# Cumulative sums stored by chunks, larger transfers, and merge loads begun by GpSimd, in a hybrid SSD and attention layer

## The chip, the cores and the metric

The kernel runs on one core of one Trainium2 chip. A core has a matrix engine (TensorE, PE, whose weight loads the profile lists as PEld), three engines that work elementwise (VectorE, DVE; ScalarE, ACT; GpSimd, POOL), and SyncE (SP), which here only begins transfers. Transfers between the chip's memory (DRAM) and the core's (SBUF) run on 16 DMA engines; any of SP, ACT and POOL can begin them, each through a queue of its own, in the order of its program. The metric is the device time of one execution in microseconds, as a median over runs.

## What is computed

One decoder layer on x of 1024 tokens by 1024 channels, in float32: a Mamba-2 branch (SSD) and a latent attention branch (MLA) side by side, merged by sigmoid gates, then a gated MLP with a short convolution.

```python
h = rms_norm(x, norm_mix_g)
z, xbc, dt_raw, q_a, kv_a, k_rope_raw, gates = split(h @ w_in)
y_ssd = ssd_mixer(z, xbc, dt_raw, ...) @ w_ssd_proj      # 32 heads in 4 groups, 8 chunks of 128 tokens
y_mla = mla_mixer(q_a, kv_a, k_rope_raw, ...) @ w_mla_proj  # 16 heads, causal
g_ssd, g_mla = split(sigmoid(gates + gate_b))
x = x + (g_ssd * y_ssd + g_mla * y_mla) @ w_o
u_gate, u_val = split(causal_conv(rms_norm(x, norm_ffn_g) @ w_up))
x = x + (silu(u_gate) * u_val) @ w_down

# in ssd_mixer, per chunk and head
a_cum = cumsum(dt * a)                                   # along the 128 tokens of a chunk
decay_in = exp(where(causal, a_cum[l] - a_cum[s], -inf))
y_diag = einsum(scores, decay_in, x * dt)
y_off = einsum(C, state before the chunk, exp(a_cum))
```

## The kernel before, in words

Matrix products are made exact enough by splitting each float32 operand into a high part (rounded to float32r) and a remainder: three matmuls (high x high, high x low, low x high; lines 174 to 176) stand for one. For weights, `load_w` brings a matrix in two halves: SP loads a half into `wraw` (two buffers, line 159), ACT casts it to `whi` (line 152), and POOL or DVE subtracts to get `wlo` (line 153). `whi` and `wlo` have two buffers too, so the loads run only a little ahead of PE. Activations (`h`) are split in the same way (lines 145 to 153).

The stages, by time in the profile:

- 0 to 100 us: norm, the small projections, and the cumulative sums of dt times a. These stand in SBUF as `acum` (tokens on partitions); a transposed copy (32 heads by 1024 tokens) goes to DRAM as `ac_d` (line 521).
- to 700 us: attention, eight pairs of heads in two halves of 512 queries. Gate and z projections are fitted in between from the table `PACE`, and stored in DRAM as `g_d` and `z_d` (line 306, out of `lt`, lines 328 and 329). The unnormalised attention output goes to `at_d`, the inverse row sums to `l_d` (line 685 ff.).
- to about 1285 us: SSD, four groups of eight chunks. For each chunk ACT begins `abc_load` (line 788), which broadcasts the chunk's cumulative sums of the group's eight heads to all 128 partitions (`abc`, 128 x 1024), and `z_load` (line 796). ACT makes the decays `seg` from `abc` (lines 850 and 852), DVE multiplies them (lines 863 to 867), PE makes the state `sn` (line 874) and the output `yp` (line 891). Besides, the convolutions (lines 808 to 816), the normalising of `at_d` by `l_d` (lines 977 to 988), and from about 1150 us on the attention projection (`mla_tiles`) run in the background: 16 tiles, each with a gate load (line 1028, into buffers `rb` or `chan`, five in turn) and a store to `m_d` (line 1035).
- to about 1570 us: the merge, in two halves of 512 tokens. For each of eight tiles `ct`, ACT begins the loads of `gt` from `g_d` and `mt` from `m_d`; PE multiplies by `w_ssd` (48 matmuls of 512 columns), DVE gates and adds (lines 1223, 1224, 1228). Then `w_o`, the residual x, and the store of `x2_d`. `w_raw` begins the loads of the first MLP weights, `ur` (512 KB each, lines 1126 and 1127), whose sums POOL makes (lines 1147 to 1150).
- to the end: the MLP.

The code is recorded first; a scheduler then sets each engine's order, and `behind(name)` adds a constraint that the last recorded instruction comes after another one of its engine. Each engine then runs its instructions in order, DMA issues included.

Of the kernel before, what the change touches and what calls it, by code (L numbers as in the profile page):

```python
# [9 lines left out]
F32 = mybir.dt.float32  # L10
# [7 lines left out]
P = 128  # L18
T = 1024
NT = T // P  # L20
# [4 lines left out]
HEADS = 32  # L25
GROUPS = 4
MH = 16
FFT = 22
# [44 lines left out]
def tile_hybrid_layer(ctx: ExitStack, tc: tile.TileContext, x, cols, cons, w_main, w_small, w_uq, w_ukv,  # L73
                      w_ssd, w_mla, w_o, w_up, w_down, out, pace=PACE):
    nc = tc.nc
# [6 lines left out]
    hp = ctx.enter_context(tc.tile_pool(name="hp", bufs=16))  # L82
    pl = ctx.enter_context(tc.tile_pool(name="pl", bufs=2, space=PSUM))

    ac_d = dram.tile([HEADS, T], F32, name="ac_d")
    at_d = dram.tile([D, T], F32, name="at_d")
    l_d = dram.tile([MH, T], F32, name="l_d")
    y_d = dram.tile([2 * D, T], F32, name="y_d")
    z_d = dram.tile([2 * D, T], F32, name="z_d")
    g_d = dram.tile([2 * D, T], F32, name="g_d")  # L90
# [35 lines left out]
    def behind(name):  # L126

        ins = nc.cur_bb.bb.instructions[-1]
        if name:
            tc.add_manual_dep(ins, name, mybir.DependencyInfo(  # L130
                mybir.DependencyClass.NoSync, mybir.DependencyReason.DATA), reason="order")
        return ins.name

    def last(engine):
        return [ins for ins in nc.cur_bb.bb.instructions if ins.engine == engine][-1].name
# [379 lines left out]
    for half in range(2):  # L515
# [2 lines left out]
        for i in range(4):  # L518
            PE.transpose(ps[0:32, i * P:(i + 1) * P], acum[:, half * 4 + i, :], ident)
        S.copy(act_[:, hs_(half)], ps[0:32, :])  # L520
    nc.sync.dma_start(out=ac_d, in_=act_)
    bctx.close()


    with tc.tile_pool(name="cp", bufs=2) as cp, tc.tile_pool(name="pss", bufs=4, space=PSUM) as pss, \
# [146 lines left out]
        def output(pr, half, accs, pv):  # L672

            ps = bank()
            for c in range(4):
                PE.matmul(ps[32 * c:32 * c + 32, 0:256], lhsT=ones[:, 0:32],
                          rhs=accs[c // 2][:, (c % 2) * 256:(c % 2) * 256 + 256], start=True, stop=True)
            ao = cp.tile([P, 512], F32, name="ao", bufs=1)
            S.copy(ao, pv)
            nc.sync.dma_start(out=at_d[pr * P:(pr + 1) * P, hs_(half)], in_=ao)  # L680
            lr = cp.tile([P, 512], F32, name="e", bufs=6)
            S.copy(lr[0:97, 0:256], ps[0:97, 0:256])
            for c in range(4):
                a = half * 512 + (c % 2) * 256
                nc.sync.dma_start(out=l_d[2 * pr + c // 2, a:a + 256], in_=lr[32 * c:32 * c + 1, 0:256])

        def chain(*gens):
            for g in gens:
# [83 lines left out]
    with tc.tile_pool(name="dp", bufs=2) as dp, tc.tile_pool(name="psx", bufs=1, space=PSUM) as psx, \  # L772
# [10 lines left out]
        def abc_load(n):  # L783

            if n < GROUPS * NT:
                g, c = divmod(n, NT)
                t = dp.tile([P, 8, P], F32, name="abc", bufs=3)
                nc.scalar.dma_start(out=t, in_=ac_d[8 * g:8 * g + 8, c * P:(c + 1) * P].partition_broadcast(P))
                abcs.append(t)

        def z_load(n):
# [181 lines left out]
        def normalize(n):  # L973


            if stores:
                nc.sync.dma_start(out=stores[0][0], in_=stores[0][1])
                stores.pop()
            if loaded:
                raw, rb, dst = loaded.pop()  # L980
                G.tensor_tensor(raw, raw, rb, op=ALU.mult)
                behind(squared[0])
                stores.append((dst, raw))
            if n < 16:
                k, s = n // 2, hs_(n % 2)
                raw = dp.tile([P, 512], F32, name="rb", bufs=3)
                rb = dp.tile([P, 512], F32, name="nb")
                nc.sync.dma_start(out=raw, in_=at_d[k * P:(k + 1) * P, s])
                for hd in range(2):
                    nc.sync.dma_start(out=rb[64 * hd:64 * hd + 64, :], in_=l_d[2 * k + hd, s].partition_broadcast(64))  # L990
                loaded.append((raw, rb, at_d[k * P:(k + 1) * P, s]))

        def mla_tiles():

            at1 = []
            count = [0]

            def at1_step(j):

                if j % 4 == 2 and 6 <= j < 38:  # L1000
                    at1.append(ordered_split(staged.pop(0)))
                if j % 4 == 0 and j < 32:
                    staged.append(raw_load(at_d, j // 4, hs_(1), lt.tile([P, 512], F32, name="lt")))

            def y_step(j):

                if 8 <= j < 16 and j % 2 == 0:
                    ya0[j // 2 - 4] = ordered_split(staged.pop(0))
                if 25 <= j:
                    ya0[j - 21] = ordered_split(staged.pop(0))  # L1010
                if j < 24 and j % 2 == 0:
                    k = j // 2
                    raw = dp.tile([P, 512], F32, name="nb") if 4 <= k < 6 else \
                        dp.tile([P, 8, P], F32, name="abc", bufs=3).rearrange("p a b -> p (a b)")[:, 0:512] if k > 8 else \
                        lt.tile([P, 512], F32, name="lt")
                    staged.append(raw_load(y_d, k, hs_(0), raw))

            def one(w, ct, half, side=None):
                s = hs_(half)

                n = turn[0] = turn[0] + 1
                gt = dp.tile([P, 512], F32, name="rb", bufs=3) if n % 5 < 3 else \
                    dp.tile([P, T], F32, name="chan", bufs=4)[:, 0:512]
                ps = lin_tile()
                for k, _ in enumerate(steps([w], (at, at1)[half], ps, range(KD), KD)):
                    if k == 2:
                        name = last(mybir.EngineType.SP)
                        nc.sync.dma_start(out=gt, in_=g_d[(8 + ct) * P:(9 + ct) * P, s])
                        behind(name)
                    if side:  # L1030
                        side(count[0])
                    count[0] += 1
                    yield True
                V.scalar_tensor_tensor(gt, gt, 1.0, ps, op0=ALU.add, op1=ALU.mult)
                nc.sync.dma_start(out=m_d[ct * P:(ct + 1) * P, s], in_=gt)

            for ct in range(4):
                w = load_w(w_mla[ct], [P, KD, P])
                if held:
                    name = last(mybir.EngineType.SP)  # L1040
                    release()
                    behind(name)
                yield from one(w, ct, 0, at1_step)
            for ct in range(4, 8):
                w = load_w(w_mla[ct], [P, KD, P])
                for half in range(2):
                    yield from one(w, ct, half, at1_step)
            count[0] = 0
            for ct in range(4):
                yield from one(load_w(w_mla[ct], [P, KD, P]), ct, 1, y_step)  # L1050
            ya0[11] = ordered_split(staged.pop(0))
# [11 lines left out]

        abc_load(0)
        ls = dp.tile([P, P], F32, name="bt")
        lv = l_d.rearrange("h (c t) -> (h c) t", t=P)
        for n, _ in enumerate(conv_group(0)):

            if n == 17:
# [50 lines left out]
    class Pair:  # L1120
        e = None

    def w_raw(q):
        q.r1 = up.tile([P, KD, P], F32, name="ur1", bufs=2)
        q.r2 = up.tile([P, KD, P], F32, name="ur2", bufs=2)
        nc.sync.dma_start(out=q.r1, in_=w_up[q.j])
        nc.sync.dma_start(out=q.r2, in_=w_up[FFT + q.j])

    def w_tiles(n, wide=True):
        if n < 2:  # L1130
# [37 lines left out]
    with tc.tile_pool(name="ep", bufs=2) as ep:  # L1168
        x2b = []
        with tc.tile_pool(name="em", bufs=2) as em:  # L1170
# [32 lines left out]
            m0 = [em.tile([P, 2, 512], F32R, name="ma", bufs=3) for _ in range(3)]  # L1203
            for half in range(2):
                if half:
                    w_raw(q0)
                    w_raw(q1)
                s = hs_(half)
                ya = ya0 if half == 0 else [load_act(y_d, k * P, s) for k in range(16)]
                ms = []  # L1210
                for ct in range(8):
                    gt = em.tile([P, 512], F32, name="gt")
                    nc.scalar.dma_start(out=gt, in_=g_d[ct * P:(ct + 1) * P, s])
                    mt = em.tile([P, 512], F32, name="mt")
                    nc.scalar.dma_start(out=mt, in_=m_d[ct * P:(ct + 1) * P, s])
                    if half == 0 and ct == 0:
                        ps = head[0]
                    else:
# [13 lines left out]
                    drain([norm(x0, x0, ep, x2ss[0])])  # L1232
                big = ep.tile([P, 4, D], F32, name="x2")
                x2b.append(big)
                for i in range(4):
                    r0 = (half * 4 + i) * P
                    nc.sync.dma_start(out=big[:, i, :], in_=x[r0:r0 + P, :])
                    behind(loaded)
                sq4 = ep.tile([P, 4, 4], F32, name="sq4")
                x2ss.append(sq4)  # L1240
                nq = 0
                for cq in range(4):
                    banks = [bank6() for _ in range(4)]
                    qs = slice(cq * 256, (cq + 1) * 256)
                    for kp in range(2):
# [12 lines left out]
                        for i in range(4):  # L1258
# [6 lines left out]
                            if kp:  # L1265
                                V.tensor_tensor(big[:, i, qs], ps, big[:, i, qs], op=ALU.add)
                                junk = em.tile([P, 256], F32, name="junk", bufs=1)
                                S.activation(junk, big[:, i, qs], AF.Square, accum_out=sq4[:, i, cq:cq + 1])
                                if half:
                                    nc.scalar.dma_start(out=x2_d[512 + i * P:512 + (i + 1) * P, qs], in_=big[:, i, qs])  # L1270
                            if half and i % 2 and nq < KD:
                                quarter("11" if nq < 4 else "21", nq % 4, h2_raw(nq, 0), act_tile(), G)
                                nq += 1
                if half == 0:
                    for i in range(4):
                        nc.sync.dma_start(out=x2_d[i * P:(i + 1) * P, :], in_=big[:, i, :])

# [374 lines left out]
```

## Time and profile before

| | |
|---|---|
| median of 3 runs | 2260.72 us (2260.71 to 2261.99) |
| the profiled execution | 2257.6 us, its span 2255.6 us |
| PE busy | 2184.2 us, 97% of the span |
| DVE, ACT, POOL busy | 1433.8, 1010.7, 758.7 us |
| SP's queue (q1) | 101232 packets, 214.73 MB |
| ACT's queue (q10) | 57520 packets, 36.84 MB |
| chain that ended last | PE 70%, DVE 16%, DMA 5%, ACT 4% |

In a row of a timeline stand the start, the duration, engine, line, operation, what it writes and reads, how many, and in brackets the engine's idle time ahead of it with what ended it. SPq and ACTq are the DMA issues of these engines. In a row of waits stand the waiting instruction, what ended the wait, the sum in us, how often, and the longest. In a row of the chain, a DMA's duration runs from its issue to its landing.

### The profile page before, as it was taken

The numbers are of one execution on the slowest core, as the hardware profiler recorded it, in microseconds if no ns is written. First come the engines' busy times: TensorE is split into PE (matmuls) and PEld (weight loads), VectorE is DVE, ScalarE is ACT, GpSimd is POOL, SyncE is SP. The second block draws the span as 40 slices with busy tenths as digits, with TensorE's granted clock in tenths as the row PEclk, the third lists the DMA queues.
The fourth block names the chain that finished last, engine by engine and source line by source line (L and its number), as shares of the span: only waits on it lengthen the run. The fifth ranks groups of instructions, "written<-read, shape, count | busy, mean of one in ns | idle before, by whom it ended". The sixth has DMA issues, their size and how long they took to land.

```text
span 2255.6 us, 31367 instructions
## 1 busy us (share of the span) xinstructions
PE 2184.2 (97%) x11488; PEld 1771.6 (79%) x11488; DVE 1433.8 (64%) x2496; ACT 1010.7 (45%) x1852; POOL 758.7 (34%) x799
## 2 busy tenths in 40 slices
PE   8999999999999999999989999999899999999999
PEld 7877777777777887777877778989778888888887
DVE  4567665667662469897966845546887767774432
ACT  5444454454443446555644424325544444443231
POOL 2244433444232235464523300003365555510000
PEclk9999999999999999999999999999999999999999
DMA  4121111111114235654367556453122222237541
GB/s 144 58 67 49 49 43 53 54 53 38 53 49 121 67 89 143 174 153 153 107 176 218 181 198 227 159 168 113 56 94 79 80 84 78 81 124 259 198 138 66
DMA packets 158905, 253.56 MB, mean 112 GB/s; under 512 B 13504, under 2 KB 68480, under 8 KB 158752
## 3 DMA queue, kind: packets, MB, share of 16 engines
q1 hardware_dynamic: 101232, 214.73, 28.2%
q10 hardware_dynamic: 57520, 36.84, 6.9%
q8 instruction: 90, 1.47, 0.3%
q14 instruction: 63, 0.52, 0.1%
HBM read 194.63 MB, written 56.89 MB: 112 GB/s over the span
## 4 chain that ended last, share of the span: by engine, by line
PE 70%; DVE 16%; DMA 5%; ACT 4%; issue 2%; POOL 1%; SPq 0%; ACTq 0%; DVEq 0%; POOLq 0%
PE lin L174 11%; PE lin L176 11%; PE lin L175 11%; PE dps L174 8%; PE dps L176 8%; PE dps L175 8%; PE pv L669 2%; DMA rb<-at_d 2%; PE s L174 1%; DVE xg L812 1%; PE s L175 1%; PE s L176 1%; PE s L626 1%; DMA wraw<-in_w_mla 1%; DVE qk L587 1%
## 5 line engine op out<-in xcount | busy, mean ns | idle before, releaser
L174 PE MATMUL lin<-h,whi 128*128 128x512 f32 x1440 | 595.4, 413 | 10.8 <-DVE lt L329 7.9
L176 PE MATMUL lin<-h,wlo 128*128 128x512 f32 x1440 | 567.4, 394 | 9.4 <-DVE wlo L153 8.2
L175 PE MATMUL lin<-h,whi 128*128 128x512 f32 x1440 | 565.8, 393 | 0.0
L174 PEld LDWEIGHTS lin<-h,whi 128*128 128x128 f32 x1440 | 273.1, 190 | 94.2 <-issue 33.7
L176 PEld LDWEIGHTS lin<-h,wlo 128*128 128x128 f32 x1440 | 272.5, 189 | 71.3 <-DVE wlo L153 9.0
L175 PEld LDWEIGHTS lin<-h,whi 128*128 128x128 f32 x1440 | 273.6, 190 | 53.3 <-issue 6.7
L152 ACT CAST whi<-wraw 128x512 fp32r<-128x512 f32 x276 | 165.2, 618 | 268.8 <-PE lin L175 110.9
L153 POOL TENSOR_TENSOR wlo<-wraw,whi 128x512 fp32r<-128x512 f32 x134 | 196.1, 1481 | 232.7 <-ACT whi L152 215.8
L658 ACT ACTIVATE e<-s 128x512 f32<-128x512 f32 (+1 forms) x192 | 93.7, 492 | 166.0 <-DVE s L656 141.3
L663 POOL TENSOR_TENSOR acc<-acc,e 128x512 f32<-128x512 f32 (+3 forms) x80 | 79.6, 994 | 232.5 <-ACT e L658 219.0
L153 DVE TENSOR_TENSOR wlo<-wraw,whi 128x512 fp32r<-128x512 f32 x142 | 99.8, 721 | 87.1 <-ACT whi L152 86.8
L153 DVE TENSOR_TENSOR h<-ar,h 128x1024 fp32r<-128x1024 f32 x40 | 48.9, 1225 | 109.3 <-ACT h L152 109.1
L152 ACT CAST h<-ar 128x1024 fp32r<-128x1024 f32 x40 | 42.2, 1054 | 125.8 <-PE lin L175 115.0
L175 PE MATMUL dps<-wlo,h 128*128 128x512 f32 x240 | 93.4, 389 | 0.0
L174 PE MATMUL dps<-whi,h 128*128 128x512 f32 x240 | 93.4, 389 | 0.0
L176 PE MATMUL dps<-whi,h 128*128 128x512 f32 x240 | 93.4, 389 | 0.0
L850 ACT ACTIVATE seg<-abc,acum 128x128 f32<-128x128 f32 x256 | 82.0, 391 | 24.8 <-PE yp L891 16.7
L812 DVE SCALAR_TENSOR_TENSOR xg<-craw,cl,xg 128x1024 f32<-128x1024 f32 x48 | 75.9, 1580 | 18.2 <-ACT xg L810 17.8
L1191 POOL TENSOR_TENSOR h<-x,h 128x512 fp32r<-128x512 f32 x8 | 11.1, 1389 | 220.9 <-ACT h L1190 220.9
L663 DVE TENSOR_TENSOR acc<-acc,e 128x512 f32<-128x512 f32 (+3 forms) x80 | 53.5, 669 | 41.3 <-ACT e L658 40.7
L1138 ACT CAST xhi<-ur 128x512 fp32r<-128x512 f32 (+1 forms) x41 | 34.1, 831 | 88.9 <-PE dps L175 80.0
L669 PE MATMUL pv<-e,vt 128*64 128x512 f32 (+3 forms) x384 | 72.9, 498 | 0.0
(581 smaller groups left out, 5179.5 us busy)
## 6 DMA issues: line engine op xcount, KB each, us to landing
wraw<-in_w_main SPq DMA_DIRECT2D x112, 256.0 KB
ur<-in_w_up SPq DMA_DIRECT2D x44, 512.0 KB
ar<-a_d SPq DMA_DIRECT2D x40, 512.0 KB
abc<-ac_d ACTq DMA_DIRECT2D x32, 512.0 KB
wraw<-in_w_ssd SPq DMA_DIRECT2D x64, 256.0 KB
wraw<-in_w_down SPq DMA_DIRECT2D x44, 256.0 KB
a_d<-uc SPq DMA_DIRECT2D x22, 512.0 KB
g_d<-lt SPq DMA_DIRECT2D x32, 256.0 KB
```

Of the source, the lines that this page charges most:

```text
L152: S.copy(hi, raw)
L153: (eng or V).tensor_sub(lo, raw, hi.bitcast(F32))
L174: PE.matmul(ps, lhsT=ah, rhs=bh, start=first, stop=False, **more)
L175: PE.matmul(ps, lhsT=ah, rhs=bl, start=False, stop=False, **more)
L176: PE.matmul(ps, lhsT=al, rhs=bh, start=False, stop=last, **more)
L587: V.tensor_tensor(qk[:, :, 2 + hd, 0:64], qk[:, :, 2 + hd, 0:64], rr[:, :, 2 + hd:3 + hd].broadcast_to([P, 4, 64]), op=ALU.mult)
L658: S.activation(e[:, c0:512], ps[:, 0:w], AF.Exp)
L663: (V if hd else G).tensor_tensor(accs[hd][:, c0:512], accs[hd][:, c0:512], e[:, c0:512], op=ALU.add)
L669: PE.matmul(pv[hd * 64:(hd + 1) * 64, c0:512], lhsT=vt[:, j, hd * 64:(hd + 1) * 64], rhs=es[hd][:, c0:512], start=first, stop=last)
L812: V.scalar_tensor_tensor(c, raw[:, k:k + T], col(cw + k), c, op0=ALU.mult, op1=ALU.add)
L850: S.activation(seg[:, hd, :], abc[:, hd, :], AF.Relu, bias=acum[:, c, 8 * g + hd:8 * g + hd + 1], scale=-1.0)
L1138: S.copy(hi, r)
```

## The change

It has six parts. `ac_d` is laid out by chunks, so that a chunk's eight rows of 128 numbers lie one behind the other; the store now scatters, and a broadcast reads one run of 4 KB for each partition, where it read eight of 512 bytes. `l_d` is laid out so that one store carries the four rows of a pair and half. The gate loads of `mla_tiles` are begun by POOL and no more by SP; the merge's loads of `gt` and `mt` by POOL and no more by ACT. The `ur` loads of the first two pairs get a constraint behind the loads of the sixth tile of the first half. x is loaded in one transfer of 2 MB for each half, where there were four of 512 KB, and `x2_d` stored in one of 2 MB (first half) or four of 512 KB (second half), where there were four of 512 KB and 16 of 128 KB.

```diff
@@ -82,9 +82,10 @@
     hp = ctx.enter_context(tc.tile_pool(name="hp", bufs=16))
     pl = ctx.enter_context(tc.tile_pool(name="pl", bufs=2, space=PSUM))
 
-    ac_d = dram.tile([HEADS, T], F32, name="ac_d")
+    ac_d = dram.tile([NT, HEADS, P], F32, name="ac_d")
     at_d = dram.tile([D, T], F32, name="at_d")
-    l_d = dram.tile([MH, T], F32, name="l_d")
+
+    l_d = dram.tile([4 * MH, 256], F32, name="l_d")
     y_d = dram.tile([2 * D, T], F32, name="y_d")
     z_d = dram.tile([2 * D, T], F32, name="z_d")
     g_d = dram.tile([2 * D, T], F32, name="g_d")
@@ -518,7 +519,7 @@
         for i in range(4):
             PE.transpose(ps[0:32, i * P:(i + 1) * P], acum[:, half * 4 + i, :], ident)
         S.copy(act_[:, hs_(half)], ps[0:32, :])
-    nc.sync.dma_start(out=ac_d, in_=act_)
+    nc.sync.dma_start(out=ac_d.rearrange("c h t -> h c t"), in_=act_.rearrange("h (c t) -> h c t", t=P))
     bctx.close()
 
 
@@ -680,9 +681,8 @@
             nc.sync.dma_start(out=at_d[pr * P:(pr + 1) * P, hs_(half)], in_=ao)
             lr = cp.tile([P, 512], F32, name="e", bufs=6)
             S.copy(lr[0:97, 0:256], ps[0:97, 0:256])
-            for c in range(4):
-                a = half * 512 + (c % 2) * 256
-                nc.sync.dma_start(out=l_d[2 * pr + c // 2, a:a + 256], in_=lr[32 * c:32 * c + 1, 0:256])
+            r0 = 4 * (2 * pr + half)
+            nc.sync.dma_start(out=l_d[r0:r0 + 4, :], in_=lr[0:128:32, 0:256])
 
         def chain(*gens):
             for g in gens:
@@ -785,7 +785,7 @@
             if n < GROUPS * NT:
                 g, c = divmod(n, NT)
                 t = dp.tile([P, 8, P], F32, name="abc", bufs=3)
-                nc.scalar.dma_start(out=t, in_=ac_d[8 * g:8 * g + 8, c * P:(c + 1) * P].partition_broadcast(P))
+                nc.scalar.dma_start(out=t, in_=ac_d[c, 8 * g:8 * g + 8, :].partition_broadcast(P))
                 abcs.append(t)
 
         def z_load(n):
@@ -987,7 +987,9 @@
                 rb = dp.tile([P, 512], F32, name="nb")
                 nc.sync.dma_start(out=raw, in_=at_d[k * P:(k + 1) * P, s])
                 for hd in range(2):
-                    nc.sync.dma_start(out=rb[64 * hd:64 * hd + 64, :], in_=l_d[2 * k + hd, s].partition_broadcast(64))
+                    r0 = 4 * (2 * k + n % 2) + 2 * hd
+                    nc.sync.dma_start(out=rb[64 * hd:64 * hd + 64, :],
+                                      in_=l_d[r0:r0 + 2, :].rearrange("a b -> (a b)").partition_broadcast(64))
                 loaded.append((raw, rb, at_d[k * P:(k + 1) * P, s]))
 
         def mla_tiles():
@@ -1024,9 +1026,7 @@
                 ps = lin_tile()
                 for k, _ in enumerate(steps([w], (at, at1)[half], ps, range(KD), KD)):
                     if k == 2:
-                        name = last(mybir.EngineType.SP)
-                        nc.sync.dma_start(out=gt, in_=g_d[(8 + ct) * P:(9 + ct) * P, s])
-                        behind(name)
+                        nc.gpsimd.dma_start(out=gt, in_=g_d[(8 + ct) * P:(9 + ct) * P, s])
                     if side:
                         side(count[0])
                     count[0] += 1
@@ -1063,7 +1063,7 @@
 
         abc_load(0)
         ls = dp.tile([P, P], F32, name="bt")
-        lv = l_d.rearrange("h (c t) -> (h c) t", t=P)
+        lv = l_d.rearrange("r (c t) -> (r c) t", t=P)
         for n, _ in enumerate(conv_group(0)):
 
             if n == 17:
@@ -1120,11 +1120,13 @@
     class Pair:
         e = None
 
-    def w_raw(q):
+    def w_raw(q, name=None):
         q.r1 = up.tile([P, KD, P], F32, name="ur1", bufs=2)
         q.r2 = up.tile([P, KD, P], F32, name="ur2", bufs=2)
-        nc.sync.dma_start(out=q.r1, in_=w_up[q.j])
-        nc.sync.dma_start(out=q.r2, in_=w_up[FFT + q.j])
+        for raw, j in ((q.r1, q.j), (q.r2, FFT + q.j)):
+            nc.sync.dma_start(out=raw, in_=w_up[j])
+            if name:
+                behind(name)
 
     def w_tiles(n, wide=True):
         if n < 2:
@@ -1203,16 +1205,16 @@
             m0 = [em.tile([P, 2, 512], F32R, name="ma", bufs=3) for _ in range(3)]
             for half in range(2):
                 if half:
-                    w_raw(q0)
-                    w_raw(q1)
+                    w_raw(q0, loaded)
+                    w_raw(q1, loaded)
                 s = hs_(half)
                 ya = ya0 if half == 0 else [load_act(y_d, k * P, s) for k in range(16)]
                 ms = []
                 for ct in range(8):
                     gt = em.tile([P, 512], F32, name="gt")
-                    nc.scalar.dma_start(out=gt, in_=g_d[ct * P:(ct + 1) * P, s])
+                    nc.gpsimd.dma_start(out=gt, in_=g_d[ct * P:(ct + 1) * P, s])
                     mt = em.tile([P, 512], F32, name="mt")
-                    nc.scalar.dma_start(out=mt, in_=m_d[ct * P:(ct + 1) * P, s])
+                    nc.gpsimd.dma_start(out=mt, in_=m_d[ct * P:(ct + 1) * P, s])
                     if half == 0 and ct == 0:
                         ps = head[0]
                     else:
@@ -1232,10 +1234,8 @@
                     drain([norm(x0, x0, ep, x2ss[0])])
                 big = ep.tile([P, 4, D], F32, name="x2")
                 x2b.append(big)
-                for i in range(4):
-                    r0 = (half * 4 + i) * P
-                    nc.sync.dma_start(out=big[:, i, :], in_=x[r0:r0 + P, :])
-                    behind(loaded)
+                nc.sync.dma_start(out=big, in_=x[s, :].rearrange("(i p) c -> p i c", p=P))
+                behind(loaded)
                 sq4 = ep.tile([P, 4, 4], F32, name="sq4")
                 x2ss.append(sq4)
                 nq = 0
@@ -1266,14 +1266,14 @@
                                 V.tensor_tensor(big[:, i, qs], ps, big[:, i, qs], op=ALU.add)
                                 junk = em.tile([P, 256], F32, name="junk", bufs=1)
                                 S.activation(junk, big[:, i, qs], AF.Square, accum_out=sq4[:, i, cq:cq + 1])
-                                if half:
-                                    nc.scalar.dma_start(out=x2_d[512 + i * P:512 + (i + 1) * P, qs], in_=big[:, i, qs])
+                                if half and i == 3:
+                                    nc.scalar.dma_start(out=x2_d[s, qs].rearrange("(i p) c -> p i c", p=P),
+                                                        in_=big[:, :, qs])
                             if half and i % 2 and nq < KD:
                                 quarter("11" if nq < 4 else "21", nq % 4, h2_raw(nq, 0), act_tile(), G)
                                 nq += 1
                 if half == 0:
-                    for i in range(4):
-                        nc.sync.dma_start(out=x2_d[i * P:(i + 1) * P, :], in_=big[:, i, :])
+                    nc.sync.dma_start(out=x2_d[s, :].rearrange("(i p) c -> p i c", p=P), in_=big)
```

On ACT the issues stay where they are, but between the first two broadcasts and the third, at the start of the SSD stage, the order around them differs. Before:

```order
L328 ACTIVATE lt<-lin 128x512
L788 DMA abc<-ac_d 128x8x128
L796 DMA zt<-z_d 128x4x128
L788 DMA abc<-ac_d 128x8x128
L328 ACTIVATE lt<-lin 128x512
L152 CAST whi<-wraw 128x512 x2
L850 ACTIVATE seg<-abc,acum 128x128 x8
L788 DMA abc<-ac_d 128x8x128
L328 ACTIVATE lt<-lin 128x512
```

After:

```order
L329 ACTIVATE lt<-lin 128x512
L788 DMA abc<-ac_d 128x1024
L796 DMA zt<-z_d 128x4x128
L788 DMA abc<-ac_d 128x1024
L850 ACTIVATE seg<-abc,acum 128x128 x3
L153 CAST whi<-wraw 128x512
L329 ACTIVATE lt<-lin 128x512
L153 CAST whi<-wraw 128x512
L850 ACTIVATE seg<-abc,acum 128x128 x5
L788 DMA abc<-ac_d 128x1024
```

Three of the eight `seg` instructions have moved ahead of the cast and of the z tile's `lt`, and the next `lt`, which stood right behind the third broadcast, comes later.

On SP, the queue from the end of the SSD stage into the merge. Before (`y_d<-xg` are the last stores of the SSD stage, `x_13408` is the residual x of the first half):

```order
L966 DMA y_d<-xg 128x512 x4
L159 DMA wraw<-in_w_ssd 128x512 x2
L1126 DMA ur_13946<-in_w_up 128x1024
L1127 DMA ur_13947<-in_w_up 128x1024
L1126 DMA ur_13950<-in_w_up 128x1024
L159 DMA wraw<-in_w_ssd 128x512 x2
L1127 DMA ur_13951<-in_w_up 128x1024
L159 DMA wraw<-in_w_ssd 128x512 x14
L1237 DMA x_13408<-in_x 128x1024 x3
```

After:

```order
L966 DMA y_d<-xg 128x512 x4
L160 DMA wraw<-in_w_ssd 128x512 x18
L1237 DMA x_13360<-in_x 128x4x1024
L160 DMA wraw<-in_w_ssd 128x512 x2
L1127 DMA ur_13892<-in_w_up 128x1024
L1127 DMA ur_13893<-in_w_up 128x1024
L160 DMA wraw<-in_w_ssd 128x512 x2
L1127 DMA ur_13896<-in_w_up 128x1024
L1127 DMA ur_13897<-in_w_up 128x1024
```

The four `ur` loads have moved behind 18 more weight loads and behind x. On DVE at the same place, before:

```order
L958 SCALAR_TENSOR_TENSOR xg<-xg,cl,np__12801 128x512 x4
L153 TENSOR_TENSOR wlo<-wraw,whi 128x512 x2
L1223 SCALAR_TENSOR_TENSOR gt<-gt,lin 128x512
L1224 TENSOR_TENSOR gt<-gt,mt 128x512
L153 TENSOR_TENSOR wlo<-wraw,whi 128x512 x2
L1228 SCALAR_TENSOR_TENSOR ma<-gt,ma 128x512
```

After:

```order
L958 SCALAR_TENSOR_TENSOR xg<-xg,cl,np__12753 128x512 x4
L154 TENSOR_TENSOR wlo<-wraw,whi 128x512 x4
L1225 SCALAR_TENSOR_TENSOR gt<-gt,lin 128x512
L1226 TENSOR_TENSOR gt<-gt,mt 128x512
L1230 SCALAR_TENSOR_TENSOR ma<-gt,ma 128x512
```

Two more weight halves stand ahead of the first `gt`. On POOL, the middle of the MLA tiles. Before:

```order
L153 TENSOR_TENSOR wlo<-wraw,whi 128x512 x2
L879 TENSOR_TENSOR st<-st,cdec 128x512
L915 TENSOR_TENSOR sq__12037<-sq__12037 128x256
L916 TENSOR_TENSOR sqs<-sq__12037 128x128
L153 TENSOR_TENSOR wlo<-wraw,whi 128x512 x2
```

After:

```order
L1029 DMA chan<-g_d 128x512
L154 TENSOR_TENSOR wlo<-wraw,whi 128x512 x2
L879 TENSOR_TENSOR st<-st,cdec 128x512
L1029 DMA rb<-g_d 128x512
L915 TENSOR_TENSOR sq__11989<-sq__11989 128x256
L916 TENSOR_TENSOR sqs<-sq__11989 128x128
L1029 DMA rb<-g_d 128x512
L154 TENSOR_TENSOR wlo<-wraw,whi 128x512 x2
```

The gate loads now stand between the weight halves and the state sums, as on SP they stood between weight loads and stores.

## The prediction, made before the changed kernel had run

> **What bounds the kernel now.** I read the page first: the span, the engines' busy time, the queues.
>
> ```profile
> span 2255.6 us, 31367 instructions
> PE 2184.2 (97%) x11488; PEld 1771.6 (79%) x11488; DVE 1433.8 (64%) x2496; ACT 1010.7 (45%) x1852; POOL 758.7 (34%) x799
> q10 hardware_dynamic: 57520, 36.84, 6.9%
> ```
>
> TensorE (PE) is busy for 2184.2 of 2255.6 us, so 71.4 us of idle time is all that better transfers can win, plus what slow matmuls cost behind a pause. The diff touches no matmul. The question is therefore which pauses of PE end on a transfer that the diff changes. Next I read the waits of PE, and its timeline for the long pauses.
>
> ```profile
> PE sn L874 <- DVE bt L863: 7.1, 5, 1.7
> PE yp L891 <- DVE seg L864: 2.8, 3, 1.3
> 719.30 0.66 PE L174 MATMUL lin<-h,whi 128*128 128x512 f32 x1 [3.02 <-DVE lt L329]
> 1167.72 0.80 PE L174 MATMUL lin<-h,whi 128*128 128x512 f32 x1 [4.92 <-DVE lt L329]
> 1187.49 0.50 PE L174 MATMUL lin<-h,whi 128*128 128x512 f32 x1 [2.15 <-ACT whi L152]
> 1188.85 0.50 PE L176 MATMUL lin<-h,wlo 128*128 128x512 f32 x1 [0.62 <-POOL wlo L153]
> 1292.26 0.50 PE L176 MATMUL lin<-h,wlo 128*128 128x512 f32 x1 [3.18 <-DVE wlo L153]
> 1316.46 0.80 PE L176 MATMUL lin<-h,wlo 128*128 128x512 f32 x1 [5.01 <-DVE wlo L153]
> ```
>
> The releaser named is only the last in a chain. The chain of waits, ScalarE's (ACT) timeline with its DMA issues, and again the chain, tell what lies behind the pauses at 719, 1167 and 1187:
>
> ```profile
> 700.31 0.39 ACTq L788 DMA_DIRECT2D abc<-ac_d  x1
> 700.73 0.61 ACTq L796 DMA_DIRECT2D zt<-z_d  x1
> 701.36 0.53 ACTq L788 DMA_DIRECT2D abc<-ac_d  x1
> 709.78 2.45 ACT L850 ACTIVATE seg<-abc,acum 128x128 f32<-128x128 f32 x8 [2.72 <-DMA abc<-ac_d]
> ...
> 704.61 12.89 DMA rb<-at_d
> 717.52 0.37 ACTq L788
> 719.96 0.43 PE lin L175
> 723.22 0.23 PE lin L174
> ...
> 1154.26 0.37 ACTq L796 DMA_DIRECT2D zt<-z_d  x1
> 1154.74 0.45 ACTq L788 DMA_DIRECT2D abc<-ac_d  x1
> 1156.72 8.76 DMA wraw<-in_w_mla
> 1174.65 0.37 ACTq L788 DMA_DIRECT2D abc<-ac_d  x1
> 1176.09 10.64 DMA wraw<-in_w_mla
> 1303.47 2.87 DMA wraw<-in_w_ssd
> ```
>
> A weight load of 256 KB takes 2.87 us at 1303.47, but 8.76 and 10.64 us where an abc load was issued 1.4 to 2.0 us ahead of it, on another queue; an at_d load takes 12.89 us behind two abc loads and a zt load. The bytes don't explain it: an abc load writes 512 KB. Its runs do: 128 partitions x 8 rows of 512 B are 1024 runs, and a zt load has 512. From 700.31 to 717.50, 2560 runs passed (17.2 us, 6.7 ns each), and from 1154.26 to 1165.48, 1536 runs (11.2 us, 7.3 ns). So I read it as about 7 ns for each run, paid one after the other, with the other queue's loads held up meanwhile. The weight halves, then the engine that splits them, then PE come late.
>
> Behind a pause of some 3 us PE is also slow: the nine matmuls from 719.30 to 723.22 take 3.92 us, where 0.23 each, as from there on, would be 2.07: 1.8 us more. The eighth column of the windows, the granted clock, shows such a loss from 1150 to 1200 (the columns before it are the busy us of PE, its weight loads, DVE, ACT and POOL; behind it stand the DMA engines' share and GB/s):
>
> ```profile
> 900.00:950.00 50.00, 47.32 (x301) 38.15 (x300) 39.06 (x58) 25.70 (x50) 24.37 (x18) 1.00 0.61 168
> 950.00:1000.00 50.00, 47.02 (x284) 36.92 (x283) 46.79 (x66) 30.86 (x60) 28.19 (x19) 1.00 0.55 155
> 1150.00:1200.00 50.00, 40.94 (x189) 31.62 (x187) 27.62 (x55) 24.43 (x49) 20.86 (x18) 0.93 0.75 221
> ```
>
> **The change, part by part.** *The layout of ac_d.* An abc load becomes 128 runs of 4 KB: 896 fewer, 6.3 us less of the shared path at 7 ns, 32 times. No row shows a broadcast of 4 KB runs. Bounds: 2.87 us (the 256 KB weight load) and 9.5 us (700.31 to 709.78, as now); I take 3.6, a quarter more than the weight load, the nearest row: as many runs (128), each twice as long. What PE gets:
> - 719: the at_d load lands before 710, ACT isn't held at 717.52. Gain 3.0 + 1.8 = 4.8; ends 0 and 4.8.
> - 1167 to 1189: the two weight loads come 6 us earlier, more than any of these pauses: 4.92 + 2.15 + 0.62 + 1.8 = 9.5 us. What is late next is the splitting of at_d tiles on ACT and VectorE (DVE), so I take 7.5; ends 4 and 9.5.
> - 900 to 1050: DVE is the tight engine (46.79 of 50 us in the second row), and lost time in the first (39.06), where ACT, which feeds it, was held by another at_d load behind abc and zt loads. The PE waits on bt and seg, 9.9 us in eight places, are that lag. I take a third, 3.3; ends 0 and 7, for a saturated DVE keeps the rest.
>
> The zt loads keep their 512 runs, so some 3.6 us of holding stays with each.
>
> *The store of ac_d* becomes 256 runs where it was 32, and GpSimd (POOL) waits for it ahead of the first query weights:
>
> ```profile
> 98.12 1.92 DMA ac_d<-act__900
> ```
>
> 224 runs x 7 ns are 1.6 us; by the code, POOL's next instructions and then the query weights' low parts follow it, so I give it little slack: +1.2; ends 0 and 3.
>
> *l_d* is stored in 16 transfers of 4 rows where there were 64 of one, and read in the same runs: 48 issues fewer on SyncE (SP), off PE's path. Nothing, with PE's work at its back; ends -1 and +0.5.
>
> *First MLP weights (ur) later, merge loads by POOL.* ACT's issues, the chain and DVE at the start of the merge:
>
> ```profile
> 1305.26 0.34 ACTq L1213 DMA_DIRECT2D gt<-g_d  x1
> 1306.36 8.27 DMA ur<-in_w_up
> 1311.38 0.69 DVE L1223 SCALAR_TENSOR_TENSOR gt<-gt,lin 128x512 f32<-128x512 f32 x1 [7.34 <-DMA ur<-in_w_up]
> 1314.66 3.43 DVE L153 TENSOR_TENSOR wlo<-wraw,whi 128x512 fp32r<-128x512 f32 x2
> ```
>
> Three loads of 512 KB stand on SP ahead of ACT's first gt; gt comes late, DVE takes its instructions in order, so the weight halves behind gt (1314.66) come late, and PE with them. After the change those halves stand ahead of gt in DVE's order, and ur behind the weight loads of six tiles. The halves can begin about 1309, before PE's work ran out at 1316.46 - 5.01 = 1311.45: gain 5.0 + 1.8 = 6.8. The first gt and mt still start only about 1305.3, with two weight loads beside them; late next is the third tile's halves behind gt. I take 6.3; ends 0 and 6.8. The ur sums on POOL now stand ahead of the last tile's loads of the half; they hold those until ur has landed. A load of ur took 8.27 us here, and it is issued about two tiles ahead (2 x 48 matmuls of 0.23 us, 22 us): nothing, ends 0 and 3.
>
> *MLA gates by POOL.* The rows of SP's waits and of the chain:
>
> ```profile
> SPq L1028 <- DMA m_d<-rb: 5.8, 1, 5.8
> SPq L1028 <- DMA m_d<-chan: 5.2, 1, 5.2
> 1280.96 4.84 DMA chan<-g_d
> 1284.93 0.83 DVE L147 TENSOR_TENSOR h<-nb,h 128x512 fp32r<-128x512 f32 x1 [1.53 <-ACT h L145]
> ```
>
> A gate load waits until its buffer's store has landed; that held SP and the weight loads behind it for 11.0 us. Now it holds POOL, and behind it there the low weight halves (wlo) and state sums. No row has a POOL issue; the nearest are SP's and ACT's, 0.33 us each. If all of both came to PE it were 11.0 + 16 x 0.33 = 16 us; of POOL's wlo PE waited for only 0.62 us at 1188.85, so I take an eighth: +2; ends 0 and 16, the upper one open, since POOL may take longer to issue. Against it, the last gates no longer stand behind y_d loads on SP: the pause at 1292 begins with 4.84 us of such a load, of which DVE idled 1.53. I take 1.5 off the 3.18; ends 0 and 4.8. The 32 loads of the merge are issued where POOL has only the ur sums to do: nothing, ends 0 and 3.
>
> *x and x2_d in larger transfers.* The same bytes and runs, but in other places. The x load of 2 MB stands ahead of two weight loads, where 1.5 MB stood, and the ur loads follow there:
>
> ```profile
> 1363.10 0.62 ACT L152 CAST whi<-wraw 128x512 fp32r<-128x512 f32 x1 [4.38 <-DMA wraw<-in_w_ssd]
> ```
>
> ACT waited 4.38 us for them and PE not at all, since it still had a full weight buffer. A third more bytes ahead are some 1.5 us: I take +0.5; ends 0 and 4. In the second half the last x2_d store carries four blocks:
>
> ```profile
> 1571.34 0.33 ACTq L1270 DMA_DIRECT2D x_d<-x  x1
> 1574.41 1.42 DVE L254 TENSOR_SCALAR x<-x,nst 128x1024 f32<-128x1024 f32 x2
> ```
>
> DVE overwrites that tile at 1574.41, 3.1 us behind the issue. 512 runs instead of 128 are 384 x 7 ns = 2.7 us more; with the 1.9 us of the ac_d store for a short one, it lands about 1571.3 + 1.9 + 2.7 = 1575.9: +1.5 (ends 0 and 3), on PE's path, since PE takes the normalised tile next.
>
> The sum: -4.8 - 7.5 - 3.3 - 6.3 - 1.5 = -23.4, and +1.2 + 2 + 0.5 + 1.5 = +5.2: -18.2. The profiled execution took 2257.6 us, the median of the runs 2260.7 is 3.1 more; I carry that over: 2260.7 - 18.2 = 2242.5.
>
> **Rivals.** (a) *A broadcast stays slow*, because one source is read 128 times whatever its runs. For it: no row shows one in longer runs. Against it: the two sums above, solved for both kinds (2048 abc runs and 512 of zt in 17.2 us, 1024 and 512 in 11.2), give 5.9 ns an abc run and 10 ns a zt run, and zt loads broadcast nothing. Were it so, the first three gains go: -6.3 - 1.5 + 5.2 = -2.6, 2258.1, no change that can be told. The Trainium skill ("DMA: Bandwidth & Descriptors", Why small descriptors are slow) gives a packet a fixed overhead of about 3 cycles, which beside the 16 beats of 512 B is an estimate of a sixth: by that rule longer runs save 1 us of 7 a load, and the time is near this rival's. The 7 ns a run in the rows speak against it.
>
> (b) *Half the gain*: the weight loads are late for bytes too (221 GB/s at 0.75 share from 1150 to 1200), and DVE keeps its lag. Half of 23.4, and 5.2 lost: -6.5, 2254.2.
>
> (c) *Slower*: POOL's queue decides. Each gate load holds the weight halves behind it until a store has landed. It cancels everything at 18.2 + 2 = 20.2 us over 16 loads, 1.3 us of PE each; at 2 us each the time is 2260.7 - 20.2 + 32 = 2272.5. For it: the waits of 5.2 and 5.8 us above, and that POOL's price for an issue is unknown. Against it: POOL is 34% busy, and on SP those waits already stood ahead of the weights. The Trainium skill ("SBUF — State Buffer", the DVE blocks DMA trap) warns that a transfer begun by GpSimd waits while DVE runs in a mode that locks their shared port; no run here shows it.
>
> **How the numbers follow.** The forecast (2228 to 2249) gets 0.56, (b) (2249 to 2256) 0.18, (a) 0.11, (c) 0.15. A measurement tells 0.2%, 4.5 us, from no change: faster is the forecast, (b) and a little of (a), 0.77; the same, most of (a) and a mild (c), 0.11; slower 0.12. The low end takes the open ends, 2.0 at 1167, 3.7 from 900 to 1050, 0.5 and 3.3 at 1316 and 1292, 1 for l_d, and no costs (5.2): 2242.5 - 15.7 = 2227. The high end reaches past (a), to 2260; beyond it lies most of (c).
>
> **What would show it.** In the changed profile the ACT queue has some 57520 - 32 x 896 - 32 x 128 = 24,750 packets; weight loads behind an abc load take 3 to 5 us; the pauses before 719, 1167, 1187 and 1316 are gone or below 1 us; the window 1150 to 1200 has PE above 46 us at a clock of 1.0. Wrong would be: PE waiting on POOL's wlo in many places, DVE on gt or rb for long, or abc loads of 8 us still.

## The result and the profile after

The changed kernel takes 2231.5 us as a median of 4 runs (2227.1 to 2234.3), the kernel before 2261.4 (2260.7 to 2262.1); the ratio is 0.9866, with an interval of 0.9847 to 0.9885. That is 30 us less, inside the range of the prediction and on the side it gave, but 12 us more than the 18 it worked out. A second set, of 6 runs against 23, has 2231.7 against 2258.2, a ratio of 0.989 (0.987 to 0.9909), or 27 us.

The page of the kernel after, to set beside the three lines of before:

```profile
span 2232.5 us, 31316 instructions
PE 2180.8 (98%) x11488; PEld 1768.4 (79%) x11488; DVE 1430.5 (64%) x2496; ACT 1013.7 (45%) x1852; POOL 779.8 (35%) x847
q10 hardware_dynamic: 24048, 28.45, 4.1%
q0 software_dynamic: 3840, 12.59, 1.8%
```

PE is idle for 51.7 us where it was 71.4, and busy for 3.4 us less, which fits its being less often slow behind a pause. ACT's queue has 24,048 packets (24,750 were forecast), and q0 is new: the loads that GpSimd begins.

PE's waits and timeline of the kernel after:

```profile
PE sn L874 <- DVE bt L863: 5.6, 3, 3.2
PE yp L891 <- DVE seg L864: 2.9, 3, 1.3
1156.22 2.08 PE L874 MATMUL sn<-xde,bt 128*128 128x512 f32 x2 [3.17 <-DVE bt L863]
1370.15 0.38 PE L175 MATMUL dps<-whi,m 128*128 128x256 f32 x1 [0.98 <-ACT m L1229]
```

The four long pauses of before (719, 1167, 1292, 1316) and the one at 1187 are gone; that at 1156 is new, and is taken up with the gates below; so is that at 1370, where PE waits in `w_o` for the last `m` that ACT makes (the prediction had no term for it). The windows show the same, those from 700 to 725 of before and then of after, and two more of after (the columns are as in the prediction):

```profile
700.00:725.00 25.00, 21.98 (x90) 17.69 (x89) 2.75 (x4) 11.71 (x27) 3.71 (x5) 0.93 0.58 158
```

```profile
700.00:725.00 25.00, 25.00 (x112) 20.68 (x112) 3.44 (x5) 12.41 (x28) 5.09 (x4) 1.00 0.74 234
900.00:950.00 50.00, 48.65 (x287) 39.55 (x288) 44.49 (x69) 29.33 (x57) 24.42 (x18) 1.00 0.58 188
1150.00:1200.00 50.00, 46.83 (x264) 36.92 (x263) 40.16 (x70) 26.95 (x56) 26.37 (x25) 0.93 0.69 227
```

From 700 to 725 the DMA engines moved 158 GB/s and now move 234, and PE has no pause at a clock of 1.00. From 900 to 950 DVE does 5.4 us more work in the same 50. From 1150 to 1200 PE is busy for 46.83 us where it was 40.94, but at a clock of 0.93, where the prediction's signs had above 46 at 1.0. An abc load lands after a median of 4.9 us, where 3.6 was taken. For the old layout such a row stands only in the run with the larger transfers alone (below); the DMA issues of that run, then of the kernel after (out<-in, how many, KB each, median us to landing):

```profile
abc<-ac_d ACTq DMA_DIRECT2D x32, 512.0 KB, 9.4
```

```profile
abc<-ac_d ACTq DMA_DIRECT2D x32, 512.0 KB, 4.9
```

### The profile page after: what moved, and what is told of

Same layout as the page of the kernel before. It is cut to its first block, busy times and chain, and to the rows that moved or that the text cites. A ratio compares the mean times of both kernels' runs of the same rounds, so it can differ in the third digit from the quotient of the medians.

```text
span 2232.5 us, 31316 instructions
## 1 busy us (share of the span) xinstructions
PE 2180.8 (98%) x11488; PEld 1768.4 (79%) x11488; DVE 1430.5 (64%) x2496; ACT 1013.7 (45%) x1852; POOL 779.8 (35%) x847
## 3 DMA queue, kind: packets, MB, share of 16 engines
q10 hardware_dynamic: 24048, 28.45, 4.1%
## 4 chain that ended last, share of the span: by engine, by line
PE 71%; DVE 16%; ACT 5%; DMA 4%; issue 2%; POOL 1%; ACTq 0%; SPq 0%; DVEq 0%; POOLq 0%
PE lin L175 12%; PE lin L177 11%; PE lin L176 11%; PE dps L175 7%; PE dps L176 7%; PE dps L177 7%; PE pv L670 2%; PE s L175 1%; DVE xg L812 1%; PE s L176 1%; PE s L177 1%; PE s L627 1%; DMA wraw<-in_w_ssd 1%; DVE chan L812 1%; DVE qk L588 1%
## 5 line engine op out<-in xcount | busy, mean ns | idle before, releaser
L812 DVE SCALAR_TENSOR_TENSOR xg<-craw,cl,xg 128x1024 f32<-128x1024 f32 x48 | 73.6, 1532 | 26.9 <-ACT xg L810 26.4
L175 PE MATMUL s<-qh,kh 97*128 97x512 f32 (+1 forms) x192 | 68.5, 357 | 2.1 <-ACT qh L644 1.2
```

The source lines that it names most:

```text
L175: PE.matmul(ps, lhsT=ah, rhs=bh, start=first, stop=False, **more)
L812: V.scalar_tensor_tensor(c, raw[:, k:k + T], col(cw + k), c, op0=ALU.mult, op1=ALU.add)
```

## The experiments

First the parts, each alone on the kernel before; then the cause of the largest. Each quoted text stood before its run. Ratios are against the kernel before on the same chip (medians of 2255.8 to 2259.1 us, by the set).

**The changed kernel again.** No edit.

> The changed kernel once more, for a second profile and for its spread. The four runs so far lie between 2227.1 and 2234.3 us, and the profiled one of 2234.3 has a pause of 3.17 us before the state matmul at 1156 us. If that pause comes and goes with how the transfers fall, the second profile has another set of short pauses between 850 and 1270 us, and its time differs by their sum and the slow matmuls behind them; if the spread comes from elsewhere, the pauses are the same in both.

2231.7 us (2230.3 to 2238.5, 6 runs). The second profile has the pause at 1157 too, of 2.84 us, and much the same short ones elsewhere. So the pause belongs to the kernel, and the spread of some 7 us comes from elsewhere. Between the two profiled executions (spans of 2232.5 and 2228.7 us) PE's idle time differs by 1.0 us, and its busy time by 4.8 (2176.0 in the second, where the clock from 1150 to 1200 was 1.00). The kernel before spreads as far (2250.0 to 2263.8 in 23 runs).

**The layout of ac_d alone.**

```diff
-    ac_d = dram.tile([HEADS, T], F32, name="ac_d")
+    ac_d = dram.tile([NT, HEADS, P], F32, name="ac_d")
-    nc.sync.dma_start(out=ac_d, in_=act_)
+    nc.sync.dma_start(out=ac_d.rearrange("c h t -> h c t"), in_=act_.rearrange("h (c t) -> h c t", t=P))
-    ... in_=ac_d[8 * g:8 * g + 8, c * P:(c + 1) * P].partition_broadcast(P)
+    ... in_=ac_d[c, 8 * g:8 * g + 8, :].partition_broadcast(P)
```

> The kernel before with the new layout of ac_d alone. If the number of runs is what costs: the pauses before 719, 1167 and 1187 go, some of the waits between 900 and 1050, and the store costs 1.2 us, so 2261 - 14 = 2247 (2243 to 2252). If a broadcast is slow whatever its runs: no gain, 2261 to 2263.

2236.2 us, 0.990 (0.988 to 0.9921): 22 us, and not 14. This part carries most of the change. Where it gains is read off from matmuls that stand in both profiles; PE's timeline of before, then with the new layout:

```profile
641.56 0.90 PE L642 MATMUL s<-nid,mc 128*97 128x128 f32 x8 [0.73 <-DVE mc L638]
906.80 0.44 PE L891 MATMUL yp<-seg,xdt 128*64 128x128 f32 x4 [1.05 <-DVE seg L864]
1024.29 0.44 PE L891 MATMUL yp<-seg,xdt 128*64 128x128 f32 x4 [1.28 <-DVE seg L864]
1276.66 0.44 PE L891 MATMUL yp<-seg,xdt 128*64 128x128 f32 x4 [0.51 <-DVE seg L864]
```

```profile
641.13 0.90 PE L642 MATMUL s<-nid,mc 128*97 128x128 f32 x8 [0.77 <-DVE mc L638]
901.47 0.44 PE L891 MATMUL yp<-seg,xdt 128*64 128x128 f32 x4 [1.04 <-DVE seg L864]
1014.49 0.44 PE L891 MATMUL yp<-seg,xdt 128*64 128x128 f32 x4 [1.27 <-DVE seg L864]
1255.22 0.44 PE L891 MATMUL yp<-seg,xdt 128*64 128x128 f32 x4 [0.49 <-DVE seg L864]
1270.58 0.79 PE L176 MATMUL lin<-h,wlo 128*128 128x512 f32 x1 [2.97 <-DVE wlo L153]
1295.91 0.80 PE L176 MATMUL lin<-h,wlo 128*128 128x512 f32 x1 [5.25 <-DVE wlo L153]
```

The lead is 0.4, 5.3, 9.8 and 21.4 us: 4.9 by 907, 4.5 more by 1024, 11.6 more by 1277. The last two rows are the pauses of before at 1292 and 1316, unchanged: the layout does nothing for them.

**Merge loads by GpSimd and the first MLP weights later, alone** (the lines of `w_raw`, its two calls, and `gt` and `mt` of the merge, as in the diff of the change).

> The kernel before with the merge loads begun by GpSimd and the first MLP weights later, nothing else. If the pause of 5.0 us at 1316 comes from the first MLP weights and the order on VectorE: 2261 - 6.5 = 2255 (2253 to 2258). If GpSimd's issues cost more than they save: no gain.

2253.1 us, 0.9978 (0.9967 to 0.9989): 5 us. The pause at 1316 is gone, those at 719 (3.23), 1169 (4.53) and 1291 (2.44) remain, and one of 1.17 at 1382 is new. DVE's timeline of this run:

```profile
1305.51 0.69 DVE L153 TENSOR_TENSOR wlo<-wraw,whi 128x512 fp32r<-128x512 f32 x1 [2.71 <-ACT whi L152]
1307.87 0.69 DVE L1225 SCALAR_TENSOR_TENSOR gt<-gt,lin 128x512 f32<-128x512 f32 x1 [0.71 <-DMA gt<-g_d]
```

The weight halves begin at 1305.51, ahead of gt, which comes at 1307.87; in the kernel before they began at 1314.66, behind gt at 1311.38. The run changes who begins gt and mt, when ur is loaded, and with both the order on DVE, so it doesn't tell how much each of them gains.

**MLA gate loads by GpSimd, alone.**

```diff
-                        name = last(mybir.EngineType.SP)
-                        nc.sync.dma_start(out=gt, in_=g_d[(8 + ct) * P:(9 + ct) * P, s])
-                        behind(name)
+                        nc.gpsimd.dma_start(out=gt, in_=g_d[(8 + ct) * P:(9 + ct) * P, s])
```

> The kernel before with the MLA gate loads begun by GpSimd, nothing else. By the prediction's terms +2 - 1.5, no change (2258 to 2264). If waiting on SyncE for a buffer's store had held the weight loads behind it (11.0 us of waits): faster by 3 to 8, 2253 to 2258. If GpSimd's queue holds its weight halves: slower, 2266 and more.

2259.7 us, 1.0005 (0.9993 to 1.0017): no change. In PE's timeline of this run the pause at 1292 has gone, and the next one and that at 1187 are longer:

```profile
1190.69 0.71 PE L174 MATMUL lin<-h,whi 128*128 128x512 f32 x1 [3.32 <-ACT whi L152]
1317.98 0.80 PE L176 MATMUL lin<-h,wlo 128*128 128x512 f32 x1 [7.08 <-DVE wlo L153]
```

5.01 us became 7.08, and 2.15 became 3.32. Together they grew by 3.24 us, and the pause that went had 3.18: it turned into other waits.

**The larger transfers alone** (`l_d`, x and `x2_d`, as in the diff of the change).

> The kernel before with the larger transfers alone (l_d, x, x2_d). By the prediction's terms +2: 2260 (2258 to 2262), of it 1.5 at the pause before the transposes at about 1575 us. By the changed kernel's profile, where that pause is shorter and not longer: 2258, no change.

2256.8 us, 0.999 (0.9981 to 0.9998): 1 us faster, not 2 slower.

The parts sum to -22.0 - 5.1 + 1.5 - 1.3 = -26.9; the whole measured -26.6 in the first of these sets. They add.

**Is it the runs or the broadcast?** Two kernels read x in place of ac_d, without a broadcast, so the decays are wrong numbers: in 1024 runs of 512 bytes, and in 128 of 4 KB.

```diff
-    ... in_=ac_d[8 * g:8 * g + 8, c * P:(c + 1) * P].partition_broadcast(P)
+    ... in_=x[:, c * P:(c + 1) * P].rearrange("(j p) t -> p j t", p=P)          # 1024 runs
+    ... in_=x[c * P:(c + 1) * P, :].rearrange("p (j t) -> p j t", t=P)          # 128 runs
```

> The kernel before, but each abc load reads 8 pieces of 512 bytes of x for each partition, others for every partition: the same 1024 runs and 512 KB, no broadcast (the decays are computed from wrong numbers). If the number of runs costs: the pauses before 719, 1167 and 1187 stay, 2258 (2253 to 2262). If the broadcast from one source costs: they go, 2236 to 2246.

> The kernel before, but each abc load reads one row of 4 KB of x for each partition: 128 runs, no broadcast (wrong numbers again). If runs cost and a broadcast doesn't: as the new layout alone, 2236 (2231 to 2240). If a broadcast of 4 KB runs costs something still: faster than that, below 2231.

2236.7 us (0.9904, 0.989 to 0.9918) and 2237.1 us (0.9909, 0.9892 to 0.9927): the same, and the same as the new layout. The first has every run of the kernel before, and none of its cost. Its page and its window, where ACT's queue has 57,520 packets as before but they took 5.4% and not 6.9%, and 234 GB/s flow and not 158:

```profile
q10 hardware_dynamic: 57520, 36.84, 5.4%
700.00:725.00 25.00, 25.00 (x112) 20.67 (x112) 3.42 (x5) 12.10 (x27) 5.09 (x4) 1.00 0.73 234
```

So 7 ns for each run is refuted. But a broadcast of 4 KB runs (the new layout) costs nothing either. Two theories were left: short runs read by all partitions are slow, or it is where the eight pieces lie, 4 KB apart in the old layout and side by side in the new.

**Where the pieces lie.** The kernel before with ac_d's rows 4608 bytes apart; and the new layout with a gap behind each head, so that the load needs 1024 runs again.

```diff
-    ac_d = dram.tile([HEADS, T], F32, name="ac_d")
+    ac_d = dram.tile([HEADS, T + P], F32, name="ac_d")          # the first kernel
+    ac_d = dram.tile([NT, HEADS, P + 32], F32, name="ac_d")     # the second, on the new layout
```

> The kernel before with the rows of ac_d 4608 bytes apart instead of 4096; the broadcasts still read eight runs of 512 bytes for each partition. If the slow part is that all pieces of a chunk lie a multiple of 4 KB apart, so that they fall on one part of the memory: fast, 2236 (2232 to 2242). If short runs of one source read by all partitions are slow wherever they lie: no change, 2258 (2254 to 2262).

> The new layout alone, but with a gap of 128 bytes behind each head's 512, so that a chunk's eight rows lie within 5 KB and each broadcast still needs 1024 runs. If the distance of the pieces matters: fast, 2236 (2232 to 2242). If the short run read by all partitions matters: slow, 2258 (2254 to 2262).

2239.3 us (0.9918, 0.9901 to 0.9935) and 2234.3 us (0.9897, 0.988 to 0.9914). Both fast, both with 1024 runs for each load, and both broadcasts. Page and windows of the first:

```profile
q10 hardware_dynamic: 57520, 36.84, 5.5%
700.00:725.00 25.00, 25.00 (x112) 20.70 (x111) 2.75 (x4) 12.10 (x27) 5.09 (x4) 1.00 0.74 233
1150.00:1200.00 50.00, 48.70 (x284) 38.48 (x284) 38.68 (x73) 29.64 (x64) 25.81 (x23) 1.00 0.82 260
```

Moving the rows of one small tensor apart by 512 bytes, and nothing else, gains 20 of the 22 us. (The store, and in the second kernel the load, address the part of each row that holds numbers; these lines are left out above.) The weight load of the first kernel behind an abc load takes 3.62 us where it took 8.76 (the chain of waits, at 1144.53 and at 1156.72 of before):

```profile
1144.53 3.62 DMA wraw<-in_w_mla
```

**Do the other tensors' rows matter, 4 KB apart as they are?** Two kernels: the changed one with each zt load as one run of 2 KB for each partition (one z tile for all four, so the gating is wrong), and the changed one with gates on SP and the rows of at_d, y_d, z_d, g_d and m_d 4608 bytes apart.

```diff
-    ... in_=z_d[4 * g * P:4 * (g + 1) * P, c * P:(c + 1) * P].rearrange("(j p) t -> p j t", p=P)
+    ... in_=z_d[4 * g * P:(4 * g + 1) * P, hs_(c // 4)].rearrange("p (j t) -> p j t", t=P)
```

```diff
-    at_d = dram.tile([D, T], F32, name="at_d")
+    at_d = dram.tile([D, T + P], F32, name="at_d")
... y_d, z_d, g_d and m_d alike
```

> The changed kernel, but each zt load reads one run of 2 KB for each partition (of one z tile, so the gating uses wrong numbers): 128 runs in place of 512, the same bytes. If runs cost, a zt load lands some 2 us earlier than its 5.5 us, and what is held behind it on the other queues too; VectorE bounds most of the pauses that are left, so 2231.6 falls by 1 to 5, to 2227 to 2231. If it is the count of bytes: 5.5 us as before and no gain.

> The changed kernel with the MLA gate loads on SyncE, and the rows of at_d, y_d, z_d, g_d and m_d 4608 bytes apart instead of 4096. Their loads read each row once, in 512 rows or 128. If rows 4 KB apart are slow to read in any load: the zt loads of 512 bytes a piece land faster and the weights behind them too, 2222 to 2226. If only a few places read again and again are slow: no change from the kernel without this padding, 2226 to 2231.

2229.4 us (0.9869, 0.9856 to 0.9883) and 2228.2 us (0.9886, 0.9867 to 0.9905). The first is inside what was expected, but doesn't tell the theories apart: a zt load lands in a median of 4.7 us where the changed kernel's second profile has 5.5, but the changed kernel with the gates on SP (below), with 512 runs, has 4.3. The second is the same as the kernel without the padding (2228.6, below). Rows 4 KB apart that are each read once cost nothing that these runs show.

**The changed kernel with the gates back on SP** (the gate diff, reversed).

> The changed kernel with the MLA gate loads back on SyncE. The parts alone sum to -22 (layout), -5 (merge and first MLP weights), -1.3 (sizes) and +1.5 (gates), so without the gates 2230 against 2231.6. By the places: the pause of 2.8 us at 1157 falls to 0.8, the one of 3 us at about 1270 comes back, 2230 to 2233. If GpSimd's gate loads are worth more in company than alone: 2234 and more.

2228.6 us (2225.8 to 2233.3), 0.9869 (0.985 to 0.9889). The two pauses trade as expected, in PE's timeline:

```profile
1155.71 1.12 PE L874 MATMUL sn<-xde,bt 128*128 128x512 f32 x2 [0.86 <-DVE bt L863]
1271.86 0.80 PE L177 MATMUL lin<-h,wlo 128*128 128x512 f32 x1 [3.58 <-DVE wlo L154]
```

3.17 us became 0.86, and 3.58 came back at 1272. Its median is 3 us below the changed kernel's of its own set and its interval overlaps that one's, so it isn't shown to be the better.

## Why the prediction was right, and where it was not

The time (inside the range), the sign and the places were right; the reason given for the largest part was wrong. Of the 8.7 us by which the parts exceed the 18.2 of the sum, the layout gives 7.6 and the larger transfers 3.3; the first MLP weights with the merge loads fall short by 1.2 and the gates by 1.0.

| term | predicted | measured |
|---|---|---|
| 719 | -4.8 | -4.9 |
| 900 to 1050 | -3.3 (0 to -7) | -4.5 |
| 1167 to 1189 | -7.5 (-4 to -9.5) | -11.6, from 1024 to 1277 |
| store of ac_d | +1.2 (0 to +3) | about 0 |
| first MLP weights, merge loads | -6.3 (0 to -6.8) | -5.1 |
| gates | +2 - 1.5 | +1.5 (-1.6 to +3.8) |
| x, x2_d, l_d | +0.5 + 1.5 + 0 | -1.3 |

*The step that failed* is "about 7 ns for each run, paid one after the other". It came from two sums over old abc and zt loads mixed; solving them for two prices used up all the evidence, and the price for zt that came out (10 ns) was taken as proof against rival (a). 1024 runs without the broadcast took no more time than 128. What the runs showed in its place: eight pieces of 512 bytes that lie 4 KB apart, all read by all 128 partitions. Take away the spacing (c1, c2), or the reading by all (b1), and it is gone; rows 4 KB apart, where each is read once, cost nothing (d1). Rival (a), that a broadcast stays slow, was wrong too. The new layout worked because it also took the pieces off their spacing of 4 KB. That is luck: by 7 ns a run the kernels b1 and c1, which keep all 1024 runs for each load, would have stayed at 2258 us, and they took 2236.7 and 2239.3. The change cut the runs and moved the pieces at once, so a wrong reason forecast the right direction and places.

All terms that were worked out as runs x 7 ns were wrong with it. The store of ac_d has 256 runs now, and GpSimd's wait for it ends as soon after its issue as before, by SP's and POOL's timelines with the new layout:

```profile
98.28 0.32 SPq L521 DMA_DIRECT2D ac_d<-act__900  x1
100.37 0.11 POOL L553 MEMSET qk<- 128x8 f32 x1 [22.47 <-DMA ac_d<-act__900]
```

That is 2.1 us, and 98.12 + 1.92 in the kernel before is the same. The last x2_d store has 512 runs, and the norm that waits for it starts 3.3 us behind its issue, against 3.1:

```profile
1546.96 0.37 ACTq L1270 DMA_DIRECT2D x_d<-x  x1
1550.26 1.42 DVE L255 TENSOR_SCALAR x<-x,nst 128x1024 f32<-128x1024 f32 x2
```

Without these two the costs of the sum are 2.5 and not 5.2.

*Mis-sized*: 1167 to 1189, where 11.6 us came back and the upper end was 9.5. The pauses that the prediction listed there, with what is slow behind the long one, make 9.5, and it left out those at 1155 and 1157 (0.74 and 0.63 us), which went too; what is left of the 11.6 wasn't traced. What was to be late next, the splitting of at_d, comes to no more than the 0.79 us that PE waits at 1155 with the new layout.

*Right*: the weight loads that came late beside abc, in order through ACT and DVE; and the pause at 1316, gone with the ur loads out of the way and the weight halves ahead of gt on DVE. One reading there was off: by SP's timeline of before the three ur loads are issued at 1305.07, 1305.44 and 1306.36, so only the first stands ahead of ACT's first gt at 1305.26. GpSimd's queue, rival (c), had no weight: an issue mostly takes POOL 0.54 to 0.58 us, some 26 us for all 48, and PE waits for POOL's wlo nowhere in the profile after, and for 0.2 us in the second one. POOL's timeline of after, and PE's waits in the second profile:

```profile
1285.02 0.58 POOL L1215 DMA_DIRECT2D gt<-g_d  x1 [16.85 <-DMA wraw<-in_w_ssd]
```

```profile
PE lin L177 <- POOL wlo L154: 0.2, 1, 0.2
```

But the gates did bring the pause at 1156 (0.79 with the layout alone, 0.86 with gates on SP, 3.17 and 2.84 with them on GpSimd), where the prediction took +2 for them: the wait came out elsewhere, and no run shows by which step. Half the gain, rival (b), was as wrong: with the padding alone the loads reach 260 GB/s from 1150 to 1200, and DVE didn't keep all of its lag (4.5 us of 9.9 came back).

The Trainium skill's rule on packets ("DMA: Bandwidth & Descriptors", Why small descriptors are slow) agrees with the 1024 plain runs that cost no more than 128 (2236.7 and 2237.1 us); that it makes longer runs worth little was right, and the layout gained for another reason. The same page of the Trainium skill (Latency and other measured facts) has a row on HBM rows at large powers of two, with a padding of a few KiB as the cure and spacings from 512 KiB up; the 4 KB of ac_d, and a cure by 512 bytes, are this case's own, and no run here has a spacing of the page's size.

*Open*: why eight places 4 KB apart are slow to read over and over, and 1024 are not; no spacing other than 4096, 4608 and 640 or 512 bytes was tried.

## What to carry to other kernels

When a small load holds up large ones, count its runs, but look as well at where its pieces lie and how often each is read, and try a padding of the rows before rearranging anything: here 512 bytes a row gained 20 of the change's 27 to 30 us. A price solved from as many sums as it has unknowns is a guess; a load of the same runs from another place would have tested it. And a transfer moved to another engine's queue may only move the wait, as the gates did here: say at which instruction it comes out.

## What was not expected of the hardware

- A broadcast of eight pieces of 512 bytes, 4096 bytes apart, to 128 partitions held a 256 KB load of another queue to 8.76 us; with the pieces 4608 bytes apart it took 3.62, and the window from 700 to 725 went from 158 to 233 GB/s, with as many packets on the queue (57,520).
- A load begun by GpSimd mostly takes 0.54 to 0.58 us of that engine's time, which counts as busy; those of 256 KB landed in a median of 3.9 to 4.4 us, where SP's weight loads of that size took 2.8 to 3.9 in the same profile.
